# A decoder layer on one core: the passage from the output projection to the first feed-forward pair ordered by a list scheduler instead of by hand

## The chip, the core and the metric

The kernel runs on one core of a Trainium2 chip. A core has a matrix engine (TensorE; PE in the profile, its weight loads PEld), three elementwise engines (VectorE or DVE, ScalarE or ACT, GpSimd or POOL) and a queue (SP) that issues transfers. Each engine works through its own queue in order; semaphores make one wait for another. The metric is the device time of the whole kernel in microseconds (us), the median of several runs. TensorE writes into eight banks of PSUM, 512 fp32 columns each.

## What is computed

One decoder layer on x (1024 tokens x 1024 channels), with shifts, scales and gates from a condition vector. The part around the change is the end of the mixer, the first layer norm and the feed-forward net:

```
x = layer_norm(ALPHA * x + gate1 * mix @ w_o, ln1_g[l], ln1_b[l])
h = x * (1.0 + scale2) + shift2
ffn = (silu(h @ w_gate) * (h @ w_up)) @ w_down
x = layer_norm(ALPHA * x + gate2 * ffn, ln2_g[l], ln2_b[l])
```

All is fp32. The feed-forward width is 2816.

## The kernel before

Each fp32 matrix product is made of three products of a high and a low part (SPLITS): ScalarE writes the high part, VectorE or GpSimd the low part as a difference. So every operand costs one ScalarE copy and one two-tensor subtraction.

**The passage.** The output projection goes by eight token tiles of 128 rows, in the order 7 to 0: 2 column halves x 8 channel blocks x 3 products of 512 columns each. The first three tiles are computed together, the other five one by one (`wo_tile`). Behind a tile come:

- `wo_evac`: two VectorE operations, residual plus PSUM;
- `layer_norm_tile`: two statistics, one aggregate and eleven small VectorE operations, then one ScalarE activation that normalises the row block;
- `region_t`: eight TensorE transposes, whose results are scaled and shifted into a staging buffer, by ScalarE, or by VectorE for the first half of tiles 1 and 0;
- `affine`: two multiplies by the norm's scale and two adds of its bias on the row block itself (it is the residual later); four of the half tiles are stored to DRAM (`z22_d`).

The feed-forward net uses a seven-product scheme on 2 x 2 blocks (Strassen's, in Winograd's form). For it the tokens are paired, tiles (7,6), (5,4), (3,2), (1,0) being regions i = 0 to 3, and each region needs four sums (`region_sums`) and seven splits into high and low (`region_split`). Weights pass through the same steps: `block_prep` (sums, on GpSimd), `block_high` (ScalarE), `block_low` (VectorE or GpSimd). Steps that share memory: the split regions overlay the projection's operands and weights, so regions 2 and 3 can't be written until the last projection tile has used these weights; blocks 4 to 7 overlay the staging buffers; blocks 0 and 1 lie where one projection weight was, blocks 2 and 3 where the last tiles' pooled channels were.

The feed-forward net goes by eleven pairs of 128 hidden columns x 2. A pair has seven gate steps, seven up steps and, for the pair before, seven down steps; a step is twelve matmuls of 512 columns. In the first pair the gate steps are done in halves of 256 columns: first for regions 0 and 1, then for regions 2 and 3. So the passage ends with seven half steps, seven half steps, and seven up steps; then the second pair starts with a down step.

**What sets the order.** Behind `pinned.update("TVAG")` four engines run in program order. In the passage that order is written out by hand: which tile's norm stands before which transposes, when a block is made, on which engine (`low(G)`, FIRST_G, REGION_G, MULTS, ADDS), and where `wo_last` cuts the last projection tile in three. In the last 14 steps `slot` puts a step's matmuls on the queue and behind them the elementwise work of the step before. The transfers (SP) are placed by the framework. PSUM is used as four single banks (`psA`) and two pairs (`psB`) in rotation.

Of the kernel before, what the change touches and what calls it, by code (L numbers as in the profile page):

```python
# [78 lines left out]
LAST_V = 2  # L79

# [6 lines left out]
class Times:  # L87
# [5 lines left out]
    def __init__(self):  # L93
        self.sbuf = [np.zeros(4096), np.full(4096, " "), np.zeros(4096), np.full(4096, " ")]
        self.psum, self.prev = {}, {}
        self.dma = 0.0
        self.fill = None
# [40 lines left out]

class Queue:
# [26 lines left out]
    def __getattr__(self, op):  # L166
        f = getattr(self.eng, op)

        def call(*a, **k):
            tm = self.times  # L170
            aps = [x for x in list(a) + list(k.values()) if hasattr(x, "tensor")]
# [25 lines left out]
def decoder_layer_kernel(  # L197
# [37 lines left out]

    def psA(nm="pa"):
        return ps_tile(ps1, "ps1", 512, 4, nm)
# [1227 lines left out]
    def layer_norm_tile(z, parts=(0, 512, 1024), affine=None, later=False):  # L1465
# [4 lines left out]
        for q, (lo, hi) in enumerate(zip(parts, parts[1:])):  # L1470
            V.bn_stats(st[:, q * 6 : (q + 1) * 6], z[:, lo:hi])
        V.bn_aggr(mv, st)
# [7 lines left out]
        if affine is None:  # L1480
            V.tensor_scalar(nm, mv[:, 0:1], -1.0, y, ALU.mult, ALU.mult)
            end = lambda: A.activation(z, z, AF.Identity, bias=nm, scale=y)
            return end if later else end()
# [10 lines left out]
    def wo_mm(pp, t, k, c):  # L1494
        for m, (a, b) in enumerate(SPLITS):
            T.matmul(pp, cat_op(k, a, t), WO[k][:, b * 1024 + c * 512 : b * 1024 + (c + 1) * 512],
                     start=(k == 0 and m == 0), stop=(k == KT - 1 and m == 2))

    def wo_evac(t, c, pp):
        z = XR[t][:, c * 512 : (c + 1) * 512]  # L1500
        V.scalar_tensor_tensor(z, z, float(np.float32(ALPHA)), pp, ALU.mult, ALU.add)
# [14 lines left out]
    def region_t(t):  # L1516

        z, i = XR[t], (7 - t) // 2
        for c in range(2):
            q = staged(i, (B11, B21, 7, B22)[2 * (t % 2) + c])  # L1520
            pt = psA("xT")
            for k in range(4):
                T.transpose(pt[:, k * P : (k + 1) * P], z[:, (4 * c + k) * P : (4 * c + k + 1) * P], ident)
            for k in range(4):
# [8 lines left out]
    def region_sums(i, which=(T1, T3, T2, T4)):  # L1533
        f = lambda b: staged(i, b)
        for b in which:
            x, y = {T1: (7, B11), T3: (B22, 7), T2: (B22, T1), T4: (B21, T2)}[b]
            (G if b == T3 else V).tensor_tensor(f(b), f(x), f(y), ALU.subtract)

    def region_split(i, which=(B11, T3, T2, B21, T1, B22, T4)):
        f = lambda b: staged(i, b)  # L1540
        for b in which:
            A.activation(TOK[:, i, b, 0:512], f(b), AF.Copy)
            (G if b in REGION_G[i] else V).tensor_tensor(TOK[:, i, b, 512:1024], f(b), f_(TOK[:, i, b, 0:512]), ALU.subtract)
# [52 lines left out]
    def load_set(n, half=None):  # L1596

        if n < len(loads):
            kind, p = loads[n]
# [26 lines left out]
    def block_prep():  # L1626
        n = pos["prep"]
        pos["prep"] += 1
        for st in steps_of(n):
            if type(st) is int:  # L1630
# [5 lines left out]
    def block_high():  # L1636
        n = pos["made"]
        pos["made"] += 1
        A.activation(block(n)[:, 0:512], quad(n, from_of(n)), AF.Copy)

    def block_low():
# [3 lines left out]
        by = G if low_by[0] else V  # L1645
        by.tensor_tensor(block(n)[:, 512:1024], quad(n, from_of(n)), f_(block(n)[:, 0:512]), ALU.subtract)
# [41 lines left out]
    def gu_step(kind, n, i0, ni, act, halves=True, turned=0):  # L1688
# [9 lines left out]
        def mm(out_, m_, ks, new):  # L1698
            w_, b = block(gu_blk[m_]), STEPS[m_][1]
            pv = out_.rearrange("p (i q) -> p i q", q=P)  # L1700
            for m, (x, y) in enumerate(SPLITS):
                for k in ks:
# [14 lines left out]
        def copy():  # L1717
            if n in (0, 2, 4):
                A.activation((t1, None, t2, None, t4)[n], ps_, AF.Copy)

        def vec():
            for q, val in outs:
                if n == 4:
# [21 lines left out]
        def act_():  # L1745
            for q, val in outs:
                if kind == "g":
# [60 lines left out]
    first = {}  # L1808
    pw = psB("wo")
    first[(7, 0)], first[(7, 1)] = pw[:, 0:512], pw[:, 512:1024]  # L1810
    pw = psB("wo")
    first[(6, 0)], first[(6, 1)] = pw[:, 0:512], pw[:, 512:1024]
    first[(5, 0)], first[(5, 1)] = psA("wo"), psA("wo")
# [16 lines left out]
    def mult(t, c, eng=G):  # L1830
        z = XR[t][:, c * 512 : (c + 1) * 512]
        eng.tensor_tensor(z, z, GR[:, c * 512 : (c + 1) * 512], ALU.mult)

    def add(t, c, eng=G):
        z = XR[t][:, c * 512 : (c + 1) * 512]
        eng.tensor_tensor(z, z, lnb[:, c * 512 : (c + 1) * 512], ALU.add)
        if t % 2 and c:
            SP.dma_start(z22_d[(7 - t) // 2], z)
# [6 lines left out]
    def wo_tile(t):  # L1845
        if t == 4:
            ps_ = psA("wo"), psA("wo")
        else:
            pw = psB("wo")
            ps_ = pw[:, 0:512], pw[:, 512:1024]  # L1850
        for c in range(2):
            for k in range(KT):
                wo_mm(ps_[c], t, k, c)
            yield
        for c in range(2):
            wo_evac(t, c, ps_[c])

    def norm(t):
        return layer_norm_tile(XR[t], later=True)


    pinned.update("TVAG")
    for t in (7, 6):
        for c in range(2):
            wo_evac(t, c, first[(t, c)])
        norm(t)()
    for c in range(2):
        wo_evac(5, c, first[(5, c)])
    wo = wo_tile(4)
    next(wo)  # L1870
    next(wo)
    next(wo, None)
    region_t(7)
    norm(5)()
    wo = wo_tile(3)
    next(wo)
    region_t(6)
    n4 = norm(4)
    affine(7)
    region_sums(0)  # L1880
    n4()
    next(wo)
# [3 lines left out]
    next(wo, None)  # L1886
    norm(3)()
    wo = wo_tile(2)
    next(wo)
# [3 lines left out]
    next(wo)  # L1893
    region_split(1)
    next(wo, None)
    load_set(0)
    norm(2)()
    region_t(3)
    affine(5)
    wo = wo_tile(1)  # L1900
    next(wo)
    next(wo)
    next(wo, None)
    pw = psB("wo")
    ps_ = pw[:, 0:512], pw[:, 512:1024]

    def wo_last(*ks):

        for k in ks:
            for m, (a, b) in enumerate(SPLITS):  # L1910
                for c in range(2):
# [263 lines left out]
```

## Time and profile before

| | |
|---|---|
| median of 3 runs | 1239.13 us (1238.67 to 1242.23) |
| profiled execution, its own time | 1238.72 us |
| its span, first to last instruction | 1236.7 us |
| TensorE busy | 1176.7 us (95%) |
| VectorE busy | 990.6 us (80%) |
| ScalarE busy | 661.4 us (53%) |
| GpSimd busy | 708.1 us (57%) |
| mean granted TensorE clock | 0.986 |

Times in the views count from the span's start. A row of the timeline gives the start, the length, the engine, the operation with its output and inputs by the program's names, how many are merged (x8), and in brackets how long the engine had been idle and what released it. Nearly all work is issued through one helper, so that the line is always L184 and one goes by the names: wo is the projection, xT the transposes, gu gate and up, dn down, res_X the row blocks, stage_W the staging buffers, hr_H split regions (and the projection's operands, which lay there before), wraw raw weights, wblk split weight blocks, gr_G the row of scales, lnb_R the row of biases. Matmuls overlap: a 512-column one shows 389 ns, though the next starts sooner, so rates are read from the starts.

### The profile page before, as it was taken

What the parts mean: (1) busy time and instruction counts of PE and PEld (TensorE: products, weight loads), DVE (VectorE), ACT (ScalarE), POOL (GpSimd) and SP (SyncE); (2) the same over time, 40 slices, a digit from 0 to 9 for tenths busy, and PEclk for the clock granted to TensorE, in tenths of its full rate; (3) what the DMA queues carried; (4) which work ended last, traced back from release to release, by engine and by line L of the source; (5) the groups of instructions that cost most, each with busy time, mean ns of one, the idle gap of its engine ahead of it and who ended that gap; (6) DMA issues with size and microseconds to landing.
All of it is one profiled execution on the core that took longest, in us unless ns stands there. A gap on an engine that the chain in (4) does not pass through costs nothing.

```text
span 1236.7 us, 16336 instructions
## 1 busy us (share of the span) xinstructions
PE 1176.7 (95%) x5631; PEld 917.1 (74%) x5631; DVE 990.6 (80%) x1758; ACT 661.4 (53%) x1346; POOL 708.1 (57%) x505
## 2 busy tenths in 40 slices
PE   8999989999989999987999999999999999999996
PEld 6766556687767567876778787787878787878775
DVE  5799998988999865677977878777776868787698
ACT  4667878787899882565342433333333333342521
POOL 0093484667033462477683847566575748486848
PEclk9999999999999999998999999999999999999998
DMA  9610167421000145001211021110212020102112
GB/s 353 253 43 17 44 221 284 168 86 60 29 16 1 37 183 190 10 9 40 97 34 68 35 69 38 65 69 34 69 35 86 35 86 34 68 35 103 69 52 119
DMA packets 32458, 103.39 MB, mean 84 GB/s; under 512 B 3572, under 2 KB 3572, under 8 KB 28792
## 3 DMA queue, kind: packets, MB, share of 16 engines
q1 hardware_dynamic: 32376, 102.36, 23.1%
q8 instruction: 44, 0.72, 0.2%
q14 instruction: 38, 0.31, 0.1%
HBM read 92.90 MB, written 9.45 MB: 83 GB/s over the span
## 4 chain that ended last, share of the span: by engine, by line
PE 38%; DVE 7%; POOL 5%; issue 2%; ACT 1%; DVEq 0%; POOLq 0%; ACTq 0%
PE gu L184 23%; PE dn L184 15%; DVE act_W L184 2%; DVE utmp_X L184 2%; POOL wraw_R L184 1%; POOL wblk_T L184 1%; POOL wraw_W L184 1%; POOL wblk_V L184 1%; DVE gtmp_V L184 1%; DVE wblk_T L184 1%; DVE hr_H L184 0%; POOL hr_H L184 0%; DVE stat_C L184 0%; DVE wblk_V L184 0%; DVE res_X L184 0%
## 5 line engine op out<-in xcount | busy, mean ns | idle before, releaser
L184 PE MATMUL gu<-hr_H,wblk_T 128*128 128x512 f32 (+1 forms) x924 | 216.1, 385 | 2.1 <-ACT gtmp_V L184 1.8
L184 PE MATMUL gu<-hr_H,wblk_V 128*128 128x512 f32 (+1 forms) x924 | 214.9, 384 | 2.0 <-ACT gtmp_V L184 1.7
L184 PEld LDWEIGHTS gu<-hr_H,wblk_T 128*128 128x128 f32 x924 | 170.7, 189 | 38.5 <-ACT gtmp_V L184 2.7
L184 PEld LDWEIGHTS gu<-hr_H,wblk_V 128*128 128x128 f32 x924 | 170.0, 188 | 38.0 <-ACT gtmp_V L184 2.1
L184 DVE TENSOR_TENSOR res_X<-res_X,dn 128x512 f32<-128x512 f32 (+1 forms) x253 | 158.4, 675 | 15.4 <-PE dn L184 15.3
L184 POOL TENSOR_TENSOR wraw_R<-wraw_R 128x512 f32<-128x512 f32 x64 | 93.9, 1475 | 45.8 <-DVE wblk_T L184 23.1
L184 POOL TENSOR_TENSOR wraw_W<-wraw_W 128x512 f32<-128x512 f32 x60 | 85.8, 1439 | 55.7 <-DVE wblk_V L184 27.4
L184 PE MATMUL pj<-ws_W,hT_H 128*128 128x512 f32 x456 | 116.0, 400 | 1.0 <-DVE ws_W L184 1.0
L184 PEld LDWEIGHTS pj<-ws_W,hT_H 128*128 128x128 f32 x456 | 82.9, 188 | 25.3 <-issue 6.9
L184 PE MATMUL dn<-wblk_T,act_W 128*128 128x512 f32 x324 | 79.3, 393 | 2.0 <-POOL wblk_T L184 1.2
L184 PE MATMUL dn<-wblk_V,act_W 128*128 128x512 f32 x324 | 78.8, 392 | 1.2 <-POOL wblk_V L184 1.2
L184 DVE TENSOR_SCALAR_CACHE_REDUCE junk_X<-keysD_T,colsD_X 128x1024 int16<-128x1024 int16 (+1 forms) x64 | 79.4, 1268 | 0.2
L184 ACT ACTIVATE wblk_V<-wraw_R 128x512 fp32r<-128x512 f32 x56 | 35.2, 629 | 80.6 <-POOL wraw_R L184 69.1
L184 ACT ACTIVATE wblk_V<-wraw_W 128x512 fp32r<-128x512 f32 x53 | 33.1, 627 | 75.6 <-POOL wraw_W L184 62.2
L184 PEld LDWEIGHTS dn<-wblk_T,act_W 128*128 128x128 f32 x324 | 60.1, 188 | 17.4 <-POOL wblk_T L184 3.9
L184 PEld LDWEIGHTS dn<-wblk_V,act_W 128*128 128x128 f32 x324 | 60.2, 188 | 16.3 <-POOL wblk_V L184 3.9
L184 POOL TENSOR_SCALAR sm_H<-sm_H,stat_X 128x896 f32<-128x896 f32 (+7 forms) x62 | 45.8, 755 | 44.1 <-DVE stat_X L184 31.5
L184 ACT ACTIVATE wblk_T<-wraw_W 128x512 fp32r<-128x512 f32 x56 | 34.9, 627 | 65.9 <-POOL wraw_W L184 53.9
L184 ACT ACTIVATE wblk_T<-wraw_R 128x512 fp32r<-128x512 f32 x52 | 32.5, 626 | 61.6 <-POOL wraw_R L184 48.9
L184 ACT ACTIVATE utmp_X<-gu 128x512 f32<-128x512 f32 x33 | 19.7, 598 | 72.9 <-PE gu L184 72.9
L184 DVE SCALAR_TENSOR_TENSOR score_X<-relu_K,const_C,score_X 128x384 f32<-128x384 f32 (+5 forms) x42 | 54.2, 1290 | 5.0 <-ACT relu_K L184 1.4
L184 ACT ACTIVATE junkA_T<-keys_T,colsA_X 128x768 bf16<-128x768 uint16 (+3 forms) x62 | 54.4, 877 | 3.8 <-DVE colsA_X L184 2.9
(316 smaller groups left out, 2697.4 us busy)
## 6 DMA issues: line engine op xcount, KB each, us to landing
mset_K<-in_wmr_dram SPq DMA_DIRECT2D x16, 1024.0 KB, 5.4
wm_K<-in_wma_dram SPq DMA_DIRECT2D x16, 512.0 KB, 9.8
wraw_R<-in_wg_dram SPq DMA_DIRECT2D x6, 1024.0 KB, 4.8
wraw_R<-in_wd_dram SPq DMA_DIRECT2D x12, 512.0 KB, 3.5
wraw_W<-in_wup_dram SPq DMA_DIRECT2D x12, 512.0 KB, 3.5
wraw_R<-in_wup_dram SPq DMA_DIRECT2D x10, 512.0 KB, 3.5
wraw_W<-in_wg_dram SPq DMA_DIRECT2D x5, 1024.0 KB, 4.7
wraw_W<-in_wd_dram SPq DMA_DIRECT2D x10, 512.0 KB, 3.5
```

Source lines behind the costliest of these rows:

```text
L184: ins_ = f(*a, **k)
```

## The change

The passage is recorded instead of issued: while `times.tape` is set, each call on an engine is put on a tape, in groups that `mark` begins (one half tile's projection products for one channel block, one norm's small operations, one split's low part). PSUM banks are virtual while recorded (`Bank`). `link` finds which group must follow which, from the memory that they touch. `order` is a list scheduler with a clock for each engine and a price for each operation: it repeatedly takes, of the groups that could start within 0.154 us of the earliest, the one with the highest key, which is the length of the longest chain behind it plus an offset from a table of 273 (from -539.5 to 529.3; mu0 -209.6, mu3 -124.9 and gr -86.5 are the multiplies of tile 0 and of tile 3 and the load of the second gate row). Groups of `tensor_tensor` on SBUF alone are free: VectorE or GpSimd is chosen for each, GpSimd handicapped by 0.801 us. GpSimd work and two-tensor VectorE work exclude each other in its clock. From the seventh step of the loop of 14 on (`TIE`), the steps' groups keep their order on each engine; the multiplies and adds do not. At the end the groups are issued in the order found, with real banks, and the engines are pinned to it. What is computed stays; the last projection tile takes its channel blocks in the order 1, 0, 2, ... one column half after the other, instead of both halves side by side.

```diff
+WO_K = {0: (1, 0, 2, 3, 4, 5, 6, 7)}
+TIE = 7
...
+TAPE_SLACK = 0.154
+TAPE_G = 0.801
+TAPE_START = {'T': 0.0, 'V': -2.4, 'A': -5.0, 'G': -6.0, 'S': -4.0}
...
+    def add(self, q, op, a, k):
+        if self.fresh or self.groups[-1].q != q:
+            g = Group(len(self.groups), q, self.kind)
+            g.free = q in "VG" and op == "tensor_tensor" and not self.tied
+            if self.tied:
+                g.preds |= {self.last[q]} if q in self.last else set()
+                self.last[q] = g.n
+            self.groups.append(g)
+            self.fresh = False
+        self.groups[-1].calls.append((op, a, k))
...
+    def order(self, start, prio, slack, bias, n_phys, held=6):
+
+        gs = self.groups
+        rank = [0.0] * len(gs)
+        for g in reversed(gs):
+            rank[g.n] = g.cost + g.late + max((rank[m] for m in g.succs), default=0.0)
+        key = [rank[g.n] + prio.get(g.kind, 0.0) for g in gs]
...
+        while ready:
+            cand = []
+            for n in ready:
+                g = gs[n]
+                t0 = ready_at[n]
+                if g.opens:
+                    if len(phys) < g.opens:
+                        continue
+                    t0 = max(t0, phys[g.opens - 1][0])
+                for q in ("V", "G") if g.free else (g.q,):
+                    t = max(t0, clock[q])
+                    if q == "G" or q == "V" and g.two:
+                        t = max(t, lock["V" if q == "G" else "G"])
+                    cand.append((t + (bias if g.free and q == "G" else 0.0), -key[n], n, q, t))
+            if not cand:
+                return None
+            m = min(cand)[0]
+            _, _, n, q, t = min((c for c in cand if c[0] <= m + slack), key=lambda c: (c[1], c[0]))
+            g = gs[n]
+            cost = g.cost
+            if g.free:
+                cost = (0.63, 1.29)[q == "G"]
...
+            g.on, g.at = q, t
+            clock[q] = end = t + cost
+            if q == "G" or q == "V" and g.two:
+                lock[q] = end
...
+def price(q, op, aps):
+
+    n = 1
+    for s_ in aps[-1 if q == "T" else 0].shape[1:] if not isinstance(aps[-1 if q == "T" else 0], Bank) else (512,):
+        n *= s_
+    if q == "S":
+        return 0.1, 2.0 + aps[0].nbytes() / 250e3
+    if q == "T":
+        return (0.116 if op == "transpose" else n * 0.000445), 0.27
+    if q == "A":
+        return (0.36 if n <= 128 else 0.09 + 0.00104 * n), 0.12
+    if q == "G":
+        return 0.03 + 0.00247 * n, 0.14
+    if op == "bn_stats":
+        return 0.62, 0.08
+    if n <= 16:
+        return 0.15, 0.08
+    return (0.34 if op == "tensor_scalar" else 0.09 + 0.00106 * n), 0.1
...
     def psA(nm="pa"):
+        if times.tape is not None:
+            return times.tape.bank()
         return ps_tile(ps1, "ps1", 512, 4, nm)
...
+    times.tape = tape
+    for t in (7, 6, 5):
         for c in range(2):
             wo_evac(t, c, first[(t, c)])
-        norm(t)()
...
+        norm(t)
+    wo_tile(4)
     region_t(7)
...
+    wo_tile(0)
+    norm(0)
+    for _ in range(4):
+        make_block()
     region_sums(2, (T3, T1, T2, T4))
-    block_high()
-    low()
     region_t(1)
...
+    for n in range(7):
+        at_once(gu_step("g", n, 0, 2, None))
     region_t(0)
...
+    region_sums(3, (T1, T2, T3, T4))
+    region_split(3, (B11, T3, T2, B21, T1, B22, T4))
     load_set(2)
...
     for n in range(14):
-        low_by[0] = n in FIRST_G
+        tape.tied = n >= TIE
         slot(gu_step("g", n, 2, 2, None) if n < 7 else gu_step("u", n - 7, 0, 4, ACTS), 1 if n < EARLY else COPY_AT.get(f"u{n - 7}", 0))
+        tape.tied = False
         for e in MULTS[n]:
-            mult(*mults.pop(0), G if e == "G" else V)
+            mult(*mults.pop(0))
             if not mults:
+                mark("gr")
                 SP.dma_start(GR, gate_d[1].to_broadcast([P, 1024]))
         for e in ADDS[n]:
-            add(*adds.pop(0), G if e == "G" else V)
+            add(*adds.pop(0))
     assert not mults and not adds
+    tape.link()
+    done, home, _ = tape.order(TAPE_START, TAPE_PRIO, TAPE_SLACK, TAPE_G, len(banks))
+    assert len(done) == len(tape.groups)
+    times.tape = None
+    times.banks.update((b_, banks[j]) for b_, j in home.items())
+    pinned.update("TVAG")
+    for n in done:
+        g_ = tape.groups[n]
+        for op, a_, k_ in g_.calls:
+            getattr({"T": T, "V": V, "A": A, "G": G, "S": SP}[g_.on], op)(*a_, **k_)
```

More of the change, by code (lines that the diff above doesn't have):

```diff
@@ L136, in done, with __init__, __getitem__, rearrange @@
                     p[0][k + 1][p[1]] = q
+class Bank:
+    def __init__(self, n, steps=()):
+        self.n, self.steps = n, steps
+    def __getitem__(self, ix):
+        return Bank(self.n, self.steps + ((lambda ap: ap[ix]),))
+    def rearrange(self, *a, **k):
+        return Bank(self.n, self.steps + ((lambda ap: ap.rearrange(*a, **k)),))
+    def real(self, banks):
+        ap = banks[self.n]
+        for f in self.steps:
+            ap = f(ap)
+        return ap
+class Group:
+    def __init__(self, n, q, kind):
+        self.n, self.q, self.kind, self.calls = n, q, kind, []
+        self.cost, self.late, self.preds, self.succs, self.opens, self.banks = 0.0, 0.0, set(), [], 0, set()
+        self.two, self.free, self.on, self.at = False, False, q, 0.0
@@ L170, in call @@
             tm = self.times
+            if tm.tape is not None:
+                return tm.tape.add(self.name, op, a, k)
+            real = lambda x: x.real(tm.banks) if isinstance(x, Bank) else x
+            a, k = [real(x) for x in a], {n_: real(x) for n_, x in k.items()}
             aps = [x for x in list(a) + list(k.values()) if hasattr(x, "tensor")]
@@ L1805, in act_op @@
         return q[t % 2][:, o : o + P]
[L1808 to L1813, printed above, removed]
+    tape = Tape()
+    banks = [psB("wo") for _ in range(2)]
+    banks = [pw[:, c * 512 : (c + 1) * 512] for pw in banks for c in range(2)] + [psA("wo") for _ in range(4)]
+    first = {(t, c): tape.bank() for t in (7, 6, 5) for c in range(2)}
+    times.banks.update(enumerate(banks[0:6]))
     for k in range(KT):
@@ L1885, in decoder_layer_kernel @@
     region_split(0, (B11, T3, T2, B21, T1, T4))
[L1886 to L1889, printed above, removed]
+    norm(3)
     region_t(4)
@@ L1892, in decoder_layer_kernel @@
     affine(6)
-    next(wo)
+    wo_tile(2)
     region_split(1)
-    next(wo, None)
     load_set(0)
-    norm(2)()
+    norm(2)
     region_t(3)
     affine(5)
[L1900 to L1911, printed above, removed]
-                    T.matmul(ps_[c], cat_op(k, a, 0), WO[k][:, b * 1024 + c * 512 : b * 1024 + (c + 1) * 512],
-                             start=(k == 1 and m == 0), stop=(k == KT - 1 and m == 2))
```

242 lines of the change are left out of this document (154 added, 88 removed).

## The prediction

> **What bounds the kernel now.** I read the page first (TensorE busy 95% of the span, so what can be won lies where it is not fed), then the table of stages, the waits and the timeline of TensorE. The rows of the table of stages hold: stretch, its length, then busy time (instructions) of PE, PEld, DVE, ACT and POOL, the granted clock, DMA share and GB/s.
>
> ```profile
> 489.60:614.40 124.80, 110.65 (x569) 93.75 (x568) 96.65 (x195) 61.06 (x127) 78.74 (x54) 0.95 0.13 47
> 614.40:674.90 60.50, 57.96 (x254) 47.32 (x253) 44.44 (x59) 23.68 (x43) 38.29 (x26) 1.00 0.15 53
> 674.90:733.10 58.20, 57.86 (x253) 46.98 (x253) 44.94 (x62) 21.55 (x39) 36.38 (x25) 1.00 0.16 55
> ```
>
> The first row is the passage that the change reorders; the second is the next feed-forward pair, the third the pair after that, which all later ones resemble. In the pairs TensorE is full at clock 1.00. In the passage it is idle for 14.1 us, and its clock falls. The waits of TensorE in the passage (total, times, longest) say for what:
>
> ```profile
> PE xT L184 <- ACT res_X L184: 7.2, 3, 3.5
> PE gu L184 <- ACT gtmp_V L184: 4.0, 3, 2.1
> PE xT L184 <- DVE stage_W L184: 2.5, 1, 2.5
> PE gu L184 <- DVE gtmp_V L184: 0.4, 2, 0.2
> ```
>
> 9.7 us of the 14.1 stand before transposes: the hand-written order has put them on TensorE's queue ahead of matmuls that were ready, and the normalised rows came late. So the passage is bound by the order of four in-order queues, not by TensorE's work.
>
> **TensorE's floor.** From its timeline:
>
> ```profile
> 488.45 3.92 PE L184 MATMUL wo<-hr_H 128*128 128x512 f32 x16 [0.69 <-DVE hr_H L184]
> ...
> 503.09 1.03 PE L184 MATMUL xT<-const_C,res_X 128*128 128x128 f32 x8
> 503.88 1.64 PE L184 MATMUL wo<-wo_V,ws_W 128*128 128x512 f32 x6
> 505.36 1.53 PE L184 MATMUL wo<-hr_H,ws_W 128*128 128x512 f32 x6
> ...
> 580.14 3.04 PE L184 MATMUL gu<-hr_H,wblk_V 128*128 128x256 f32 x24
> ...
> 598.11 5.60 PE L184 MATMUL gu<-hr_H,wblk_V 128*128 128x512 f32 x24
> 603.55 5.60 PE L184 MATMUL gu<-hr_H,wblk_T 128*128 128x512 f32 x24
> ...
> 614.43 1.98 PE L184 MATMUL dn<-wblk_T,act_W 128*128 128x512 f32 x8
> ```
>
> Twenty-four 512-column matmuls take 603.55 - 598.11 = 5.44 us, 0.2267 each. Between 488.45 and the first down matmul at 614.43, 125.98 us, lie the 16 of the first row, 5 tiles x 48 and 7 up steps x 12: 340 x 0.2267 = 77.1. The gate's two half steps are 2 x 7 x 12 = 168 of 256 columns, at half of 0.2267: 19.0. Eight transposes and six matmuls take 505.36 - 503.09 = 2.27, less 6 x 0.2267 is 0.91, so the 64 transposes take 7.3. Sum 103.4. So 22.6 us are there at most: 14.1 idle and 8.5 of slow matmuls. Of these 1.1 stay at any order (580.14: 24 in 3.04, 0.120 each and not 0.113, x 168). The other 7.4 are the clock:
>
> ```profile
> 564.60:568.00 3.40, 0.00 (x0) 0.00 (x0) 1.87 (x10) 1.24 (x2) 3.40 (x4) 0.84 0.01 1
> 568.00:573.00 5.00, 2.42 (x10) 2.02 (x11) 3.26 (x7) 1.04 (x3) 0.97 (x1) 0.50 0.30 104
> 573.00:582.00 9.00, 8.76 (x58) 8.55 (x57) 4.72 (x8) 6.63 (x16) 6.13 (x5) 0.77 0.17 58
> 594.00:614.00 20.00, 20.00 (x95) 16.79 (x96) 19.28 (x22) 6.48 (x13) 13.80 (x9) 1.00 0.33 107
> ```
>
> After 3.4 idle us the granted clock is 0.50 for 5 us and 0.77 for 9 more; shorter stalls should cost less of it. I let 1.5 of the 7.4 stay (bounds 0 and 7.4). [...]
>
> **Part by part.** Removed: the hand order. Added at run time: nothing; the list is worked out when the kernel is built, and no instruction is added; what more handoffs between engines cost is in the last term below. The recording, the marks and the virtual PSUM banks cost nothing on the chip. Moved: everything on TensorE, VectorE, ScalarE and GpSimd between the last of the first three tiles' matmuls and the last up step, and the issues of their DMAs (weight sets, four stores of rows, the gate row). Two things matter.
>
> First, VectorE and GpSimd. Rows of their timelines, and two groups of the same operation:
>
> ```profile
> 504.26 1.29 POOL L184 TENSOR_TENSOR res_X<-res_X,gr_G 128x512 f32<-128x512 f32 x1 [19.43 <-PE xT L184]
> ...
> 509.51 1.28 POOL L184 TENSOR_TENSOR stage_W<-stage_W 128x512 f32<-128x512 f32 x1
> ```
> ```profile
> 598.45 0.41 DVE L184 TENSOR_TENSOR gtmp_V<-gtmp_V,gu 128x256 f32<-128x256 f32 x1
> ...
> 608.46 0.69 DVE L184 TENSOR_TENSOR utmp_X<-utmp_X,gu 128x512 f32<-128x512 f32 x1 [0.61 <-ACT utmp_X L184]
> ...
> 613.58 0.68 DVE L184 TENSOR_TENSOR wblk_T<-wraw_R,wblk_T 128x512 fp32r<-128x512 f32 x1
> 614.19 0.68 DVE L184 TENSOR_TENSOR wblk_T<-wraw_W,wblk_T 128x512 fp32r<-128x512 f32 x1
> ```
> ```profile
> L184 DVE TENSOR_TENSOR hr_H<-stage_W,hr_H 128x512 fp32r<-128x512 f32 x10 | 13.2, 1342 | 10.8 <-ACT hr_H L184 10.6
> ```
> ```profile
> L184 POOL TENSOR_TENSOR hr_H<-stage_W,hr_H 128x512 fp32r<-128x512 f32 x18 | 26.7, 1506 | 11.3 <-ACT hr_H L184 11.1
> ```
>
> An operation on two SBUF tensors takes VectorE 614.19 - 613.58 = 0.61 alone, and GpSimd (509.51 - 504.26) / 4 = 1.31 (four in a row). Side by side both stretch: the same split runs 1.34 and 1.51 on average. So I count them as excluding each other. And the chain of the last tile, which also prices VectorE's other work:
>
> ```profile
> 560.92 1.27 DVE L184 SCALAR_TENSOR_TENSOR res_X<-res_X,wo 128x512 f32<-128x512 f32 x2
> ...
> 562.72 1.27 DVE L184 BATCH_NORM_STATS2 stat_C<-res_X 128x6 f32<-128x512 f32 x2
> 564.02 0.21 DVE L184 BATCH_NORM_AGGREGATE stat_C<-stat_C 128x2 f32<-128x12 f32 x1
> 564.27 2.46 DVE L184 TENSOR_SCALAR stat_C<-stat_C 128x1 f32<-128x1 f32 x11
> ...
> 570.28 1.36 DVE L184 TENSOR_SCALAR stage_W<-xT,const_C 128x128 f32<-128x128 f32 x4
> ```
> ```profile
> 566.76 1.24 ACT L184 ACTIVATE res_X<-res_X,stat_C 128x1024 f32<-128x1024 f32 x1 [2.90 <-DVE stat_C L184]
> ```
> ```profile
> 553.05 5.97 PE L184 MATMUL wo<-hr_H,plT_T 128*128 128x512 f32 x18
> ...
> 568.05 1.12 PE L184 MATMUL xT<-const_C,res_X 128*128 128x128 f32 x4 [3.54 <-ACT res_X L184]
> ```
>
> A tile costs VectorE 1.27 + 1.27 + 0.21 + 2.46 = 5.21 in 16 instructions. Eight tiles, eight small ones at 0.34 and nine that read PSUM (6 x 0.41, 3 x 0.69) are 145 of its 195 instructions, 48.9 us; the other 50 and GpSimd's 54 are the two-tensor kind, 104. With k of them on GpSimd the exclusive time is 0.61 x (104 - k) + 1.31 x k = 63.4 + 0.70 k, and VectorE's own 112.3 - 0.61 k. Today's k = 54 makes 101 us of exclusive time; k = 37 makes both 90. The list holds the two apart in its model and picks the engine per step, so it can come near 90, under TensorE's 103.4 by 14. [...]
>
> Second, the handover behind the last tile. Its matmuls end at 559.0; its transposes start at 568.05, and the second gate half (580.14) 21 us behind the tile. The list may set the remaining first-half gate steps there: 84 x 0.120 = 10.1, and tile 1's transposes 0.9. The chain itself is one evacuation 0.64, one half's statistics 0.64, 2.67, 1.24, transposes 0.9, four scalings of 0.34 and a copy of 0.6: 8.1, with handoffs some 9.5. It would be covered, but the operand blocks of tiles 2 and 3 overlay the projection's weights and can't be written until the last tile is nearly through, and gate blocks 4 to 6 overlay their staging. That puts 7 splits and 5 block lows, 12 two-tensor operations, beside that tile's 5.2 on VectorE: with three on GpSimd 5.2 + 9 x 0.61 = 10.7 us, for gate steps due within 9. I let 2 us stay (0 to 4).
>
> The list is only as good as its prices. It gives the 12 small operations of a layer norm 0.15 each, 1.8; the rows say 2.67. Eight times 0.87 makes VectorE 7.0 us later than the list thinks, and in an in-order queue all behind it: later splits, later scalings. Of that 3 us reach TensorE, I take, since VectorE has 14 us to spare but not in the stretch behind the last tile (0 to 7.0). For the rest (gate and up steps now waiting 4.4) I let 2.5 stay (0 to 4.4).
>
> What stays: 1.1 + 1.5 + 2 + 3 + 2.5 = 10.1. The passage goes from 126.0 to 113.5, 12.5 less. The next pair, 60.5 where 58.2 is the rule, I leave as it is. Against the profiled execution (1238.72 us, span 1236.7, the 2.0 outside unchanged) that is 1226.2; the median of the runs lies 0.4 above it, so 1226.6.
>
> **The rivals.** *A, the two elementwise engines stay the bound.* For it: 101 us of exclusive time today, and 28 us of VectorE's passage idle at both ends of dependencies. If the list keeps k near 54, 101 plus the 8 us before the first normalised rows plus 11 of such waits is 120: 6 less than now, 1233. The other extreme, k near 0, is VectorE's 112.3 plus the 8, the same 120. Against: the list prices the exclusion.
>
> *B, given back.* In 594 to 614 VectorE is busy 19.28 of 20, much of it with the multiplies and adds of the first norm. A shorter up phase pushes some 10 us of that into the next pair, where VectorE has 60.5 - 44.4 = 16 free, but ahead of block lows in its queue. If TensorE pays for them, 10 of the 12.5 are lost: 1236, no change. The same if the list merely reproduces today's waits.
>
> *C, slower: the gate row.* The first down step needs a block multiplied by the second gate row, which is loaded over the first norm's scale row, after the last of 16 multiplies.
>
> ```profile
> 598.78 3.15 DVE L184 TENSOR_TENSOR res_X<-res_X,gr_G 128x512 f32<-128x512 f32 x2
> ```
> ```profile
> 604.02 0.40 SPq L178 DMA_DIRECT2D gr_G<-gate_d  x1
> ```
> ```profile
> 608.40 1.30 POOL L184 TENSOR_TENSOR wraw_R<-wraw_R,gr_G 128x512 f32<-128x512 f32 x1 [5.31 <-DMA gr_G<-gate_d]
> ```
>
> The last multiply ends at 601.9, the first down matmul is at 614.4, 12.5 later; 2.1 of that the load's issue stands behind the stores of rows on SP's queue, which wait for adds, and a weight load behind a late store would wait as well. In the list the multiplies of tile 0 have priority -209.6, of tile 3 -124.9, the row's load -86.5: they come when nothing else fits. If they end VectorE's backlog, at 489.6 + 90 + 7 + 28 (its idle time today) = 614.6, the down step starts at 627.1: 12.7 later than now, 1252. It decides from a last multiply ending after some 605.6. Against: the list takes what can start first and uses priority only inside 0.154 us, and it knows the load's length (2.0 + 524 KB at 250 per us = 4.1).
>
> **How the numbers follow.** A measurement of this kernel can tell about 0.3%, 3.7 us. Forecast 0.60, A 0.14, B 0.13, C 0.13. Faster is forecast and A, 0.74; same is B, 0.13; slower C, 0.13. The forecast's own bounds: all costs at their lower ends leave 1.1, 21.5 less, 1217.6; at their upper ends 1.1 + 7.4 + 4 + 7.0 + 4.4 = 23.9 would eat all 22.6, but they hardly come together; with the largest alone at its end 16.0 stay, 6.6 less, 1232.5. The range takes in A and B and leaves out C: 1217 to 1241.
>
> **What would show it.** Right: first down matmul near 602, TensorE's waits before transposes under 3 us, no clock row under 0.8, fewer than 54 instructions on GpSimd in the passage, their means nearer 1.3. Wrong: a wait of the first down step on a gate block (C); block-low waits in the second row's stretch, longer than 60.5 (B); VectorE or GpSimd without a gap and TensorE waiting on them (A).

## The result, and the profile after

The changed kernel took 1231.97 us in the median (1231.1 to 1232.99), the kernel before 1239.08 beside it: ratio 0.9937, 95% interval [0.9919, 0.9956]. That is 7.1 us less, where 12.5 were forecast. The profiled execution of the changed kernel took 1231.1 us, with a span of 1229.0. All operations still go through one helper, now line L408, and all PSUM tiles of the list are called wo in its trace, the transposes (inputs const_C, res_X) and the gate and up steps (input wblk) too.

From the table of stages of the changed kernel, cut at 492.24, where the list's first matmul starts, at 606.67, where the first down matmul starts, and behind the next pair. The columns are as in the prediction.

```profile
492.24:606.67 114.43, 105.81 (x557) 88.36 (x556) 100.75 (x229) 63.25 (x127) 33.08 (x20) 0.99 0.13 44
606.67:667.00 60.33, 58.09 (x255) 47.48 (x254) 44.24 (x59) 23.87 (x43) 38.23 (x26) 1.00 0.15 53
```

In the kernel before the same stretch is:

```profile
492.21:614.43 122.22, 108.07 (x557) 91.62 (x556) 94.19 (x191) 61.06 (x127) 78.74 (x54) 0.94 0.12 41
```

The passage is 7.8 us shorter, all that was won; the next pair is as long as it was. GpSimd has 20 instructions instead of 54, VectorE 38 more, and VectorE is now busy for 100.75 of 114.43 us. Below, "the passage" is this stretch, from the list's first matmul to the first down matmul. The work upstream of it ends between 492 and 497 us in one profile and another, so lengths are compared, not end times. Behind the first down matmul every profile has 621.5 to 622.7 us left (its span less that start), so what an order wins or loses lies in the passage. Each length comes from one execution.

The waits of TensorE in the passage of the changed kernel (total, times, longest):

```profile
PE wo L408 <- ACT res_X L408: 3.6, 4, 2.1
PE wo L408 <- ACT gtmp_V L408: 1.5, 1, 1.5
PE wo L408 <- POOL stage_W L408: 1.5, 1, 1.5
PE wo L408 <- DVE hr_H L408: 0.8, 1, 0.8
PE wo L408 <- ACT wblk_T L408: 0.5, 1, 0.5
PE wo L408 <- ACT stage_W L408: 0.5, 1, 0.5
```

8.4 us are left of 14.1. The waits for rows, before transposes, fell from 9.7 to 3.6. Where they lie shows in the table of stages of the same kernel, cut finer:

```profile
492.24:524.00 31.76, 29.94 (x142) 24.10 (x140) 30.07 (x79) 17.07 (x36) 11.39 (x8) 1.00 0.06 22
524.00:537.00 13.00, 10.00 (x44) 8.18 (x45) 11.52 (x29) 7.44 (x15) 7.82 (x4) 0.87 0.01 2
537.00:562.00 25.00, 23.94 (x113) 18.98 (x111) 22.98 (x53) 16.00 (x35) 8.24 (x6) 1.00 0.03 11
562.00:580.00 18.00, 15.32 (x108) 13.88 (x109) 16.67 (x38) 11.48 (x22) 4.25 (x3) 1.00 0.17 59
580.00:606.67 26.67, 26.60 (x153) 23.23 (x153) 19.51 (x34) 11.26 (x23) 1.38 (x1) 1.00 0.32 110
```

Up to 580 VectorE is busy 30.07 + 11.52 + 22.98 + 16.67 = 81.2 of 87.8 us, more than TensorE (79.2). Every wait of TensorE falls there. Behind 580 TensorE runs full. So the list has packed VectorE, and the question for the runs was whether VectorE now sets the end.

### The profile page after: what moved, and what is told of

It reads as the page before. It is cut to its first block, busy times and chain, and to the rows that moved or that the text cites. A ratio compares the mean times of both kernels' runs of the same rounds, so it can differ in the third digit from the quotient of the medians.

```text
span 1229.0 us, 16334 instructions
## 1 busy us (share of the span) xinstructions
PE 1174.6 (96%) x5631; PEld 913.5 (74%) x5631; DVE 995.5 (81%) x1792; ACT 663.8 (54%) x1346; POOL 662.6 (54%) x471
## 4 chain that ended last, share of the span: by engine, by line
PE 59%; DVE 16%; ACT 9%; POOL 8%; issue 5%; DMA 3%; SPq 0%; DVEq 0%; POOLq 0%; ACTq 0%
PE gu L408 22%; PE dn L408 15%; PE pj L408 7%; PE wo L408 5%; PE pair L408 3%; DVE stat_C L408 2%; ACT sm_H L408 2%; DVE act_W L408 2%; DVE utmp_X L408 1%; DVE res_X L408 1%; PE lg L408 1%; PE iq L408 1%; DVE score_X L408 1%; POOL wraw_W L408 1%; POOL wraw_R L408 1%
## 5 line engine op out<-in xcount | busy, mean ns | idle before, releaser
L408 PE MATMUL gu<-hr_H,wblk_T 128*128 128x512 f32 x852 | 203.2, 390 | 1.1 <-ACT gtmp_V L408 0.9
L408 PE MATMUL gu<-hr_H,wblk_V 128*128 128x512 f32 x828 | 197.6, 390 | 2.0 <-ACT gtmp_V L408 1.8
L408 PEld LDWEIGHTS gu<-hr_H,wblk_T 128*128 128x128 f32 x852 | 159.5, 188 | 36.2 <-POOL wblk_T L408 1.9
L408 PEld LDWEIGHTS gu<-hr_H,wblk_V 128*128 128x128 f32 x828 | 155.0, 188 | 36.1 <-ACT gtmp_V L408 2.2
L408 DVE TENSOR_TENSOR res_X<-res_X,dn 128x512 f32<-128x512 f32 (+1 forms) x253 | 158.4, 674 | 15.4 <-PE dn L408 15.3
L408 POOL TENSOR_TENSOR wraw_W<-wraw_W 128x512 f32<-128x512 f32 x60 | 85.8, 1437 | 61.9 <-DVE wblk_V L408 27.4
L408 PE MATMUL pj<-ws_W,hT_H 128*128 128x512 f32 x456 | 116.0, 400 | 1.0 <-DVE ws_W L408 1.0
L408 POOL TENSOR_TENSOR wraw_R<-wraw_R 128x512 f32<-128x512 f32 x57 | 83.0, 1463 | 43.8 <-DVE wblk_T L408 21.8
L408 PEld LDWEIGHTS pj<-ws_W,hT_H 128*128 128x128 f32 x456 | 82.9, 188 | 25.2 <-issue 6.9
L408 PE MATMUL dn<-wblk_T,act_W 128*128 128x512 f32 x324 | 79.3, 393 | 1.6 <-POOL wblk_T L408 1.2
L408 PE MATMUL dn<-wblk_V,act_W 128*128 128x512 f32 x324 | 78.9, 392 | 1.1 <-POOL wblk_V L408 1.1
L408 DVE TENSOR_SCALAR_CACHE_REDUCE junk_X<-keysD_T,colsD_X 128x1024 int16<-128x1024 int16 (+1 forms) x64 | 79.5, 1268 | 0.2
L408 ACT ACTIVATE wblk_V<-wraw_R 128x512 fp32r<-128x512 f32 x56 | 35.1, 627 | 73.4 <-POOL wraw_R L408 61.7
L408 ACT ACTIVATE wblk_V<-wraw_W 128x512 fp32r<-128x512 f32 x53 | 33.1, 628 | 76.3 <-POOL wraw_W L408 62.9
L408 PEld LDWEIGHTS dn<-wblk_T,act_W 128*128 128x128 f32 x324 | 60.1, 188 | 17.1 <-POOL wblk_T L408 3.9
L408 PEld LDWEIGHTS dn<-wblk_V,act_W 128*128 128x128 f32 x324 | 60.2, 188 | 16.3 <-POOL wblk_V L408 4.0
L408 ACT ACTIVATE wblk_T<-wraw_W 128x512 fp32r<-128x512 f32 x56 | 34.9, 627 | 65.9 <-POOL wraw_W L408 53.9
L408 POOL TENSOR_SCALAR sm_H<-sm_H,stat_X 128x896 f32<-128x896 f32 (+7 forms) x62 | 46.0, 761 | 43.6 <-DVE stat_X L408 31.4
L408 ACT ACTIVATE wblk_T<-wraw_R 128x512 fp32r<-128x512 f32 x52 | 32.6, 628 | 59.7 <-POOL wraw_R L408 47.6
L408 POOL TENSOR_TENSOR wraw_R<-wraw_R,gr_G 128x512 f32<-128x512 f32 x24 | 35.0, 1462 | 51.9 <-DMA wraw_R<-in_wd_dram 51.9
L408 DVE SCALAR_TENSOR_TENSOR score_X<-relu_K,const_C,score_X 128x384 f32<-128x384 f32 (+5 forms) x42 | 54.1, 1288 | 5.0 <-ACT relu_K L408 1.4
L408 ACT ACTIVATE junkA_T<-keys_T,colsA_X 128x768 bf16<-128x768 uint16 (+3 forms) x62 | 54.4, 877 | 3.8 <-DVE colsA_X L408 2.9
## 6 DMA issues: line engine op xcount, KB each, us to landing
wm_K<-in_wma_dram SPq DMA_DIRECT2D x16, 512.0 KB, 10.1
```

The lines of the kernel that those rows point to most:

```text
L408: ins_ = f(*a, **k)
```

## The experiments

**Norms shortened and lengthened in the list's order.** My theory: the rest of the expected gain is lost because VectorE's norms run 2.61 us where the list believes 1.8, and nearly all of that reaches TensorE. The rival: it is lost in handoffs and the clock, whatever VectorE does. Three kernels change four small operations of each norm, 8 x 4 x 0.2175 = 7.0 us of VectorE, and nothing else: left out in the list's order, issued twice there, and left out in the hand-written order.

```diff
+        for j_, (op, a_, k_) in enumerate(g_.calls):
+            if g_.kind[:2] == "ln" and j_ in (7, 8, 9, 10):
+                continue
```
```diff
+        if g_.kind[:2] == "ln":
+            calls = calls[0:11] + calls[7:11] + calls[11:]
```
```diff
...
-        for _ in range(3):
+        for _ in range(steps):
...
-        return layer_norm_tile(XR[t], later=True)
+        return layer_norm_tile(XR[t], later=True, steps=1)
...
```

> The list's order kept step for step, but each of the eight first norms issues eight small VectorE operations instead of twelve (two of three Newton steps left out, so the norm is less exact). A norm then takes VectorE about 1.75 us, which is the 1.8 that the list had counted. Theory (VectorE is the bound of the passage and runs late by its norms): 8 x 0.87 = 7 us of lateness are gone, and nearly all of it reaches TensorE: 5 to 7 us less than the changed kernel, 1225 to 1227 us, first down matmul near 601. Rival (the lateness comes from VectorE and GpSimd clashing, or from waits that the list doesn't know): under 2 us less.

> The list's order kept, each first norm issues sixteen small operations instead of twelve (two Newton steps repeated). Theory (VectorE is the bound): 8 x 0.87 = 7 us more on VectorE, 5 to 7 us more in all, 1237 to 1239 us. Rival (clashes or unknown waits, with slack on VectorE): under 2 us more.

> The kernel before, its order by hand kept, with the same eight small operations a norm instead of twelve (norm less exact). Theory (the hand order waits on chains, and VectorE has 28 us idle there): only the norms whose rows TensorE waits for count, three or four x 0.87: 2 to 4 us less than before, 1235 to 1237. Rival (short norms help any order alike): as much as they help the list's order.

Rows of the table of stages over the passage, of the short, then of the long variant of the list's order, then of the short one of the hand order:

```profile
492.08:600.21 108.13, 103.11 (x557) 87.52 (x556) 94.60 (x197) 63.18 (x127) 33.78 (x20) 1.00 0.13 46
```
```profile
493.00:617.72 124.72, 108.94 (x557) 90.54 (x556) 110.99 (x261) 63.23 (x127) 29.05 (x20) 0.96 0.12 40
```
```profile
496.73:617.49 120.76, 106.26 (x558) 91.04 (x556) 86.34 (x152) 61.16 (x127) 78.11 (x54) 0.96 0.12 40
```

Seven us less on VectorE make the passage 6.3 shorter, seven more make it 10.3 longer; VectorE's busy time moves by as much (6.2 less; 10.2 more, where the operations added are 7.0). The ratios are 0.9871 [0.985, 0.9892] and 1.0018 [1.0002, 1.0034], around the change's 0.9937: 8.2 us less and 10.0 more. In the list's order VectorE's time is passed on to the end about one to one. In the hand-written order the same cut gives 0.9965 [0.9951, 0.9978], 4.3 us by the medians, and a passage only 1.5 shorter than 122.22. So it seems to be worth less there, but the intervals of the two gains in the medians overlap. One rival is left by these runs: a shorter norm also brings its rows sooner, whatever the load of VectorE. The next run adds load and leaves the norms as they are.

**All on VectorE.** Does GpSimd help at all?

```diff
+        g_.on = "V" if g_.free else g_.on
```

> The list's order kept, but all operations that may run on either engine go to VectorE at the place where they stood: 19 more on VectorE. Theory (VectorE is the bound): 19 x 0.61 = 11.6 us more on it, less the 1 to 2 us of clashes that go, so 6 to 10 us more in all, 1238 to 1242 us. Rival (the two engines clash so much that GpSimd's share is worth nothing): no change or faster than the changed kernel.

Its row of the table of stages over the passage:

```profile
494.00:616.12 122.12, 107.61 (x557) 89.72 (x556) 108.32 (x248) 63.53 (x127) 1.36 (x1) 0.97 0.12 41
```

Ratio 0.9993 [0.9977, 1.0009]: with the list's order but without GpSimd the whole gain is gone. GpSimd's part is needed, and load on VectorE lengthens the passage one to one (7.7 us) with unchanged norms too. But the 19 steps moved (the twentieth instruction was never the list's to place: it belongs to the last seven of the 14 steps, the eighth to the fourteenth, whose order is kept) add 108.32 - 100.75 = 7.6 us to VectorE, 0.40 each, and not 0.61: the other 0.21 is what a step on GpSimd had cost VectorE, most likely in stretched operations (groups below).

**More on GpSimd.** The prediction's figure, 37 instructions there, the order again kept.

```diff
+        g_.on = "G" if g_.n in (44, 47, 48, 49, 52, 86, 90, 102, 104, 105, 106, 107, 108, 128, 132, 204, 212) else g_.on
```

> The list's order is kept as it is, but 17 of the 76 two-tensor steps that it left on VectorE go to GpSimd (multiplies and adds of tiles 7 and 6, eight sums and splits of regions 0 and 1, two weight lows), so that k rises from 20 to 37, the figure of the prediction. The passage was 114.43 us with the list's own choice (k = 20) and 122.12 with k = 0, 0.38 us for each step moved, not 0.61. If every step moved relieves VectorE of its 0.61 (the prediction's 112.3 - 0.61 k), VectorE's busy time in the passage falls from 101.2 to about 91 and the passage by 7 to 10 us, to 104.5 to 107.5. If the two engines stretch each other as VectorE's and GpSimd's rows side by side suggest (a replay of this order in which an overlapped VectorE operation goes at half speed), the passage falls by some 2.6 us, to about 112, ratio near 0.991. If what a GpSimd step costs beyond that (a starved GpSimd operation of 5.9 us, and TensorE or ScalarE waiting for its result) grows with their number, the passage gets longer than 114.4, ratio above 0.9937.

(VectorE had 77 such steps, not 76.) Ratio 0.9938 [0.9919, 0.9957], no gain. Its row of the table of stages, and the longest wait of TensorE from its timeline:

```profile
493.36:608.96 115.60, 106.02 (x558) 89.41 (x556) 99.23 (x212) 63.31 (x127) 53.24 (x37) 0.97 0.12 43
```
```profile
548.35 1.97 PE L408 MATMUL wo<-const_C,res_X 128*128 128x128 f32 x8 [4.74 <-ACT res_X L408]
```

17 more steps on GpSimd, put there by hand in an order not made for them, took VectorE from 100.75 to 99.23, 0.09 each, and the passage got 1.2 longer. The two timelines of this kernel, GpSimd's and then VectorE's, show why:

```profile
527.61 6.94 POOL L408 TENSOR_TENSOR hr_H<-stage_W,hr_H 128x512 fp32r<-128x512 f32 x4
```
```profile
531.62 6.87 DVE L408 TENSOR_TENSOR res_X<-res_X,lnb_R 128x512 f32<-128x512 f32 x4
538.41 3.48 DVE L408 TENSOR_TENSOR hr_H<-stage_W,hr_H 128x512 fp32r<-128x512 f32 x2
541.82 1.27 DVE L408 SCALAR_TENSOR_TENSOR res_X<-res_X,wo 128x512 f32<-128x512 f32 x2
```

Here, where both have two-tensor work queued, they go in step, one of each per 1.7 us. VectorE alone does two in 1.22. So a step on GpSimd costs there more than it saves, and the next norm, queued behind on VectorE (541.82), comes late: the 4.74 us wait. What does not suffer is shown by the groups of the kernel with all on VectorE and of the changed kernel (columns: busy us, mean ns, idle before):

```profile
L408 DVE SCALAR_TENSOR_TENSOR res_X<-res_X,wo 128x512 f32<-128x512 f32 x16 | 10.5, 680 | 4.4 <-PE wo L408 4.4
L408 DVE TENSOR_TENSOR stage_W<-stage_W,stage_W 128x512 f32<-128x512 f32 x8 | 5.5, 687 | 0.2
```
```profile
L408 DVE SCALAR_TENSOR_TENSOR res_X<-res_X,wo 128x512 f32<-128x512 f32 x16 | 10.4, 678 | 4.4 <-PE wo L408 4.4
L408 DVE TENSOR_TENSOR stage_W<-stage_W,stage_W 128x512 f32<-128x512 f32 x6 | 6.1, 1018 | 0.2
```

In the changed kernel, where GpSimd works too, this two-tensor group goes from 687 to 1018 ns, the one that reads PSUM stays (680 and 678). In the rows of the run with 37 instructions a pair takes 1.7 us, where 0.61 and 1.31 one after the other are 1.92: there the two run nearly one after the other, and only a little overlaps.

**Better prices, other tables.** If the wrong price of the norm is the loss, a right one should win it back: the price alone (0.2175 for 0.15), and two searches of the table of offsets with prices taken from the trace and start times for the first evacuations.

```diff
...
-                cost = (0.63, 1.29)[q == "G"]
+                cost = (0.61, 1.31)[q == "G"]
...
-        return 0.15, 0.08
+        return 0.2175, 0.08
...
```

> One number of the list changed: a small VectorE operation priced 0.2175 us instead of 0.15 (2.61 a norm instead of 1.8, as the trace has it); offsets and all else as in the changed kernel, so the list finds another order. Played through with the true price, the old order ends its up steps 5.1 us later than the list had thought, the new one 0.9 us later than the old list's plan. Theory (the wrong price makes the plan unkeepable, and VectorE, the bound, gets more than it can do): 3 to 5 us less than the changed kernel, 0.990 to 0.9915 of before, and GpSimd given 27 pieces instead of 21. Rival (the offsets were fitted to the old price, so that another order is as bad or worse): no change or slower than the changed kernel.

> The list with prices from the trace (small VectorE operation 0.2175, a two-tensor operation 0.61 and 1.31, ScalarE copy 0.545, 256-column matmul 0.12), with the first three tiles' sums available in the order 7, 6, 5 as they are, and with new offsets found by a search that also wants the end early when costs vary. The plan ends 1.1 us later than the changed kernel's plan, and plays through with varied costs 4 to 5 us earlier than that one's. Theory: 4 to 6 us less than the changed kernel, 0.989 to 0.991 of before; the version to beat both. Rival (what is left comes from what no price holds, the clock and waits that the framework adds): under 2 us less.

> As the other searched list, from another start of the search: an order of its own with the same plan. Theory: within 2 us of the other searched list, since the prices and not a lucky order decide. Rival (luck of one order): more than 3 us between the two.

| kernel | ratio to before | passage, us | VectorE busy in it, us |
|---|---|---|---|
| the change | 0.9937 [0.9919, 0.9956] | 114.43 | 100.75 |
| price only | 0.9925 [0.9897, 0.9953] | 113.96 | 99.04 |
| searched_a | 0.9926 [0.9904, 0.9949] | 112.76 | 99.23 |
| searched_b | 0.9911 [0.9888, 0.9934] | 111.67 | 97.00 |

The row of searched_b:

```profile
493.44:605.11 111.67, 104.33 (x558) 87.68 (x557) 97.00 (x221) 63.02 (x127) 34.02 (x25) 1.00 0.13 44
```

The price alone wins 0.5 us of the passage, a new table 1.7 and 2.8, where 3 to 5 and 4 to 6 were expected. The ratios' intervals all overlap that of the change, so in the total the gain of the best is likely, not certain. A wrong price was not the main loss: VectorE has that work to do whatever the list believes. These three orders have 25 or 26 instructions on GpSimd, and VectorE is 1.5 to 3.8 us less busy than with the 20 of the change: in an order made for them, a few steps more on GpSimd seem to help.

**A table that lets the two overlap.** The list forbids two-tensor work on both engines at a time. Would it be better to let them overlap, at a price? The other prices are those of the searched tables, and the offsets were searched again.

```diff
...
-                    if q == "G" or q == "V" and g.two:
-                        t = max(t, lock["V" if q == "G" else "G"])
...
+            if q == "G":
+                cost += 0.4 * max(0.0, min(lock["V"] - t, 0.7))
+            elif q == "V" and g.two and lock["G"] > t:
+                cost = min(2 * cost, cost + 0.5 * (lock["G"] - t))
...
```

> The list with the prices of searched_a and searched_b, but with the exclusion of VectorE and GpSimd taken out of its model: an operation that overlaps one of the other engine is stretched instead (VectorE at half speed while GpSimd works, a GpSimd operation by up to 0.28 us), and the table of offsets searched again for that. The plan puts 44 steps on GpSimd and ends 106.0 us after the start; searched_a's plan ended at 105.9 and the chip took 112.8. If the exclusion was the wrong model and this one is nearer, the passage comes within some 3 us of its plan, 106 to 109, ratio 0.985 to 0.988. If handoffs and starved GpSimd operations that no price holds set the end, it is 111 to 115 like the other searched tables, ratio 0.990 to 0.994, or longer since more work is on GpSimd.

Ratio 0.9965 [0.9949, 0.9982], passage 118.70, with 43 instructions on GpSimd. Like plans on paper, 106.0 against searched_a's 105.9, came out 6 us apart on the chip. As far as one table for the one model and two for the other can show it, the list's exclusion is the better model.

**The head of the list, and eight scalings on ScalarE.** The list evacuates tile 5 first, and its first row block is ready late (VectorE's first operation starts at 491.76 where it started at 489.68 before). One run puts the first ten VectorE operations back into the hand order's sequence, tile 7 first; another takes VectorE's eight scalings of transposed rows to ScalarE, with a new table.

```diff
+    head = [n for n in done if tape.groups[n].kind in ("we7", "st7", "we6", "st6", "we5")]
+    at_ = sorted(done.index(n) for n in head)
+    head.sort(key=lambda n: (("we7", "st7", "we6", "st6", "we5").index(tape.groups[n].kind), n))
+    for i_, n in zip(at_, head):
+        done[i_] = n
```
```diff
...
-                if c == 0 and t < 2:
-                    V.tensor_scalar(dst, pt[:, k * P : (k + 1) * P], s_, b_, ALU.mult, ALU.add)
...
```

> The changed kernel's order, but VectorE's first ten operations (evacuations and statistics of tiles 7, 6, 5) in the order in which the sums are finished: tile 7 first. VectorE can then start 2.1 us earlier, at 489.7 instead of 491.8. Theory (VectorE is the bound all through the passage): 1.5 to 2.5 us less than the changed kernel, 0.992 of before. Rival (TensorE has enough to do there, the lateness arises later): no change.

> As searched_b, but the eight scalings of transposed rows that VectorE had (first half of tiles 1 and 0) go to ScalarE, which is busy 63 of some 115 us, and the table of offsets is searched again with the same prices and the same exclusion. VectorE gets 8 x 0.34 = 2.7 us less; the plan ends at 105.7, as that of searched_b. If VectorE sets the end, the passage falls by 2 to 3 us, to some 109, ratio near 0.989. If it doesn't, or if the different table weighs more than the work moved, it comes out with the other searched tables, 111 to 113, ratio 0.991 to 0.993.

Neither helped: 0.9929 [0.9905, 0.9953] with a passage of 114.19, and 0.9923 [0.9904, 0.9943] with 114.49. At the head TensorE has other matmuls, so VectorE's lateness there is free. With the scalings gone VectorE was still busy 100.91 us in the passage, 3.9 more than in searched_b, with 22 instructions on GpSimd instead of 25, and the first down matmul waited 3.55 us for it. So the new table gave VectorE more than the scalings took away, and the run doesn't tell what these alone are worth.

**Right prices and short norms.** Is VectorE still the bound in the best order? The same four operations of each norm are left out of searched_b, by the first of the edits above.

> The order of searched_b (ratio 0.9911, passage 111.67 us, its plan 105.8) with two of the three Newton steps of each of the eight norms not issued: 32 VectorE operations of 0.2175, 7.0 us, are left out, so the normalised rows are less exact. In the order of the change the same cut took 6.3 us off the passage and 0.0066 off the ratio. If VectorE still sets the end of the passage once the prices are right, the passage falls by 5 to 7 us, to 105 to 107, ratio near 0.985. If the right prices gave VectorE slack and the 5.9 us by which searched_b misses its plan come from handoffs and slower matmuls, the passage falls by at most 2 us, to 110 or 111, ratio 0.989 to 0.991.

Its row of the table of stages over the passage:

```profile
492.38:600.71 108.33, 104.23 (x557) 87.81 (x556) 90.09 (x189) 62.98 (x127) 34.63 (x25) 1.00 0.14 46
```

Ratio 0.9873 [0.9852, 0.9894]; the passage is 3.3 us shorter than that of searched_b, between the two expectations. Both orders end at 108 us once VectorE has 7 us less (108.13, 108.33). So some 108 us seems to be what is left of this passage whichever of the two orders it has, and above it VectorE costs 6.3 us in the order of the change and 3.3 in searched_b's. Whether VectorE has a part in the 108 too was not tried: no run took more off it.

## Why the prediction was right in kind and too high by 5 us

**Right: the mechanism.** TensorE's idle time in the passage was what there was to win, and the list won 5.7 of 14.1 us of it; the other 2.1 of the 7.8 us are faster matmuls (clock 0.94 before, 0.99 after). The stated range, 1217 to 1241, is wide and takes in A and B, so that the result lies in it says little; it lies between the forecast and A.

**Wrong in size.** The passage was put at 103.4 of work plus 10.1 that stay; it is 118.18 counted from 488.49, the changed kernel's counterpart of 488.45, so 14.8 stay. Taken apart by kind, in us, from the same start, where "clock" is the busy time times what the granted clock lacks of 1, in stretches of 1 us:

| | before | the change | its short norms |
|---|---|---|---|
| above the work of 103.4 | 22.6 | 14.8 | 8.5 |
| TensorE idle | 14.1 | 8.6 | 5.0 |
| lost to the clock | 5.0 | 1.7 | 0 |
| slow at full clock | 3.5 | 4.5 | 3.5 |

Two steps failed.

*"Of that 3 us reach TensorE".* Seven us off VectorE win 6.3, where the prediction had 3 for VectorE's lateness and 1.5 for the clock, and the 6.3 take in both: with short norms the clock is 1.00. The 3 rested on "VectorE has 14 us to spare", and that on the list being able to "come near 90" on VectorE, with 37 instructions on GpSimd. It took 20, and VectorE was busy for 101. The lateness wasn't that of a wrong price either, for the right price won 0.5 us of the passage; it is the load. The formula 112.3 - 0.61 k leaves out that operations staying behind are stretched (687 to 1018 ns in the group above). That it fits for 20 (100.1 against 100.75) is luck: for 1 it gives 111.7 and for 37 it gives 89.7, and the rows have 108.32 and 99.23. By the prediction's count both engines can end at 90 only if VectorE's other 48.9 us are due just when GpSimd works, and the order with 37 didn't make them so. A list searched with the exclusion for 37 was not tried.

*"The other 7.4 are the clock".* Of the 8.5 us of slow matmuls before, 5.0 are the clock and 1.1 the gate's half steps, which the prediction let stay. The last 2.4 run at full clock; they were no gain to be had, the prediction had no term for them, and after the change they are 3.4. An estimate from the rows: in front of each of the nine waits the last matmul counts as busy for 0.389 us, 0.16 longer than the 0.2267 in which the next could have started, 1.5 in all. Where the rest comes from was not traced.

**The other terms.** The clock: 1.5 taken, 1.7 measured. In the timeline of TensorE and the table of stages of the changed kernel:

```profile
521.73 2.20 PE L408 MATMUL wo<-hr_H,ws_W 128*128 128x512 f32 x9
524.94 1.09 PE L408 MATMUL wo<-const_C,res_X 128*128 128x128 f32 x8 [1.01 <-ACT res_X L408]
528.09 1.09 PE L408 MATMUL wo<-const_C,res_X 128*128 128x128 f32 x8 [2.06 <-ACT res_X L408]
528.94 1.39 PE L408 MATMUL wo<-hr_H,ws_W 128*128 128x512 f32 x3
```
```profile
529.00:530.00 1.00, 1.00 (x5) 0.84 (x4) 1.00 (x3) 1.00 (x4) 0.00 (x0) 0.61 0.09 16
530.00:531.00 1.00, 1.00 (x4) 0.71 (x4) 1.00 (x3) 0.97 (x4) 0.57 (x1) 0.50 0.00 0
531.00:532.00 1.00, 1.00 (x4) 0.81 (x3) 1.00 (x2) 1.00 (x5) 1.00 (x1) 0.50 0.03 8
532.00:533.00 1.00, 1.00 (x5) 0.78 (x4) 1.00 (x3) 0.97 (x3) 1.00 (x1) 0.68 0.00 0
```

0.39 + 0.50 + 0.50 + 0.32 = 1.7 us are lost. Against the forecast there is a clock row under 0.8, though no wait is longer than 2.06. The idle time, 8.6, is near what the prediction let stay for waits (2 + 3 + 2.5 = 7.5). Without VectorE's 6.3 us, 8.5 are left, where 1.1 + 2 + 2.5 = 5.6 were taken; searched_b's order with short norms says the same: 108.33 is 8.6 above the work of 103.4 - 16 x 0.2267 = 99.8, at clock 1.00, and its waits sum to 3.9. One wait in this that the prediction did not think of, in the timelines of the changed kernel:

```profile
511.16 0.96 PE L408 MATMUL wo<-hr_H,ws_W 128*128 128x512 f32 x3 [1.47 <-POOL stage_W L408]
```
```profile
509.84 1.26 POOL L408 TENSOR_TENSOR stage_W<-stage_W 128x512 f32<-128x512 f32 x1 [0.90 <-PE wo L408]
```

The matmul stands 1.47 us until GpSimd has written stage_W. In the program it reads other columns of the memory that the two share, so the list has no link there, but the framework sets a wait. How much such waits cost together was not tried.

**The rivals.** A, the elementwise engines stay the bound: this is what holds the gain down, with 20 instructions on GpSimd instead of 54 or none. Its sign, VectorE all but without a gap, is there up to 580 us (81.2 of 87.8), and its 1233 is nearer to the result than 1226.6. The truth lies between A and the forecast. B, given back: false, the next pair takes 60.33. C, the gate row: false. VectorE's last multiply, the load's issue and the first down matmul in the changed kernel:

```profile
589.47 1.28 DVE L408 TENSOR_TENSOR res_X<-res_X,gr_G 128x512 f32<-128x512 f32 x2
```
```profile
590.79 0.32 SPq L402 DMA_DIRECT2D gr_G<-gate_d  x1
```
```profile
606.67 1.98 PE L408 MATMUL dn<-wblk_T,act_W 128*128 128x512 f32 x8
```

The multiplies end at 590.75, before the 605.6 from which C would decide, and the first down matmul at 606.67 waits for nothing. **The signs named:** the down matmul came at 606.67 and not near 602, the waits before transposes are 3.6 and not under 3, and GpSimd's mean is 33.08 / 20 = 1.65 us, above the 1.46 of before; only the number of its instructions, fewer than 54, came as named.

## What to carry to other kernels

When a scheduler evens out the waits of the bound engine, look at once which other engine it has filled, and shorten that engine's work by a known amount in the same order: the response (here 6.3 us for 7.0) says what correcting prices can't. Two engines that stretch each other on one kind of operation, as here (1.7 us for a pair, 0.61 and 1.31 alone), are to be counted per pair: a step moved took 0.40 us off VectorE for each of the first 19 and 0.09 for each of 17 more in the same order. Between 0.991 and 0.994 the intervals of the tables overlap, and like plans on paper came out up to 6 us apart, so a plan is worth only what the profile and the runs show.

## What was not expected of the hardware

GpSimd was held up once, it seems, for much longer than one operation of VectorE, which is 0.61 us. In the timelines of the changed kernel, GpSimd's first:

```profile
530.43 5.91 POOL L408 TENSOR_TENSOR stage_W<-stage_W 128x512 f32<-128x512 f32 x1 [5.10 <-ACT stage_W L408]
536.42 1.30 POOL L408 TENSOR_TENSOR stage_W<-stage_W,stage_W 128x512 f32<-128x512 f32 x1
```
```profile
528.48 2.49 DVE L408 TENSOR_TENSOR res_X<-res_X,gr_G 128x512 f32<-128x512 f32 x4
530.89 2.49 DVE L408 TENSOR_TENSOR res_X<-res_X,lnb_R 128x512 f32<-128x512 f32 x4
533.30 1.89 DVE L408 TENSOR_TENSOR hr_H<-stage_W,hr_H 128x512 fp32r<-128x512 f32 x3
```

An operation that takes 1.3 us alone took 5.91 and ended at 536.34, 1.15 us behind VectorE's run of eleven two-tensor operations, which kept its full pace (2.41 for four). In the run with 37 instructions the two went in step instead. What decides between the two patterns the runs don't tell.

The clock fell to 0.50 with no idle time over 2.06 us, behind 5.0 us, from 523.9 to 528.94, in which TensorE ran only 16 transposes. Other rows have much the same without a fall, or the fall behind a shorter time. First the kernel with the corrected price alone, with the clock behind the wait:

```profile
532.30 2.23 PE L408 MATMUL wo<-const_C,res_X 128*128 128x128 f32 x16 [2.15 <-ACT res_X L408]
```
```profile
534.00:535.00 1.00, 1.00 (x8) 0.91 (x7) 1.00 (x2) 0.97 (x4) 0.00 (x0) 1.00 0.00 0
535.00:536.00 1.00, 1.00 (x6) 0.78 (x5) 1.00 (x3) 1.00 (x3) 0.67 (x1) 1.00 0.00 0
```

There 2.15 us idle and 16 transposes, 4.1 us without another matmul, left the clock at 1.00. Then a wait of the same 2.06 us without transposes, in the kernel before and in the hand order with short norms, each with a row of the clock behind it:

```profile
591.97 1.69 PE L184 MATMUL gu<-hr_H,wblk_W 128*128 128x256 f32 x12 [2.06 <-ACT gtmp_V L184]
```
```profile
593.00:594.00 1.00, 0.83 (x7) 0.63 (x6) 1.00 (x3) 0.20 (x1) 1.00 (x1) 1.00 0.00 0
```
```profile
593.97 7.36 PE L184 MATMUL gu<-hr_H,wblk_W 128*128 128x256 f32 x36 [2.06 <-ACT gtmp_V L184]
```
```profile
595.00:596.00 1.00, 1.00 (x6) 1.00 (x6) 1.00 (x3) 0.19 (x1) 1.00 (x1) 0.50 0.00 0
```

It left the clock at 1.00 in the one and halved it in the other. So neither the length of an idle time nor the time without another matmul decides alone here, and 0.50 came behind 2.06 idle us as it did behind the 3.40 of the kernel before. What decides was not shown, and no run here changed the transposes alone.
